# Hybrid decoder layer: projections of the third and fourth head's blocks bound to later scores, output halves interleaved

## The chip, the cores and the metric

The kernel runs on one core of a Trainium2 chip. The metric is the device time of one execution in microseconds, as the median of several executions of the same program. TensorE (PE) multiplies, VectorE (DVE), ScalarE (ACT) and GpSimd (POOL) do the element-wise work, and SyncE (SP) issues the DMA transfers.

## The reference

One layer of a decoder on a sequence of 1024 tokens of width 1024, all in float32: a joint projection, two groups of attention heads side by side, an output projection, a normalisation, and a dense SwiGLU network with its own normalisation. Cut to what matters:

```python
h = x @ w_in[l]                                    # queries, keys, values of both groups, gates
# differential attention, 4 heads: two score maps for each head
s = einsum('bqhcd,bkhcd->bhcqk', q_blk, k) * scale - slopes * dist
p = masked_softmax(s, dist >= 0)
a = p[:, :, 0] - lam * p[:, :, 1]                  # the blend of the two maps
o_diff = rms_norm(einsum('bhqk,bkhe->bqhe', a, v), subln_g) * (1 - lam_init)
o_nsa = gates[0] * o_cmp + gates[1] * o_sel + gates[2] * o_win
mix = concatenate([o_diff, o_nsa]) @ w_out[l]
x = layer_norm(DEEPNORM_ALPHA * x + mix, ln1_g[l], ln1_b[l])
ffn = (silu(x @ w_gate[l]) * (x @ w_up[l])) @ w_down[l]
x = layer_norm(DEEPNORM_ALPHA * x + ffn, ln2_g[l], ln2_b[l])
```

## The kernel before

Projections and the feed-forward products are computed in three passes: every operand is split into a high and a low part (ScalarE casts the high part on line L81, VectorE or GpSimd subtracts it on L83), and `mm3` multiplies high by high, high by low and low by high (L116 to L118). Weights that are to be split land in `big` or `w` tiles; GpSimd splits most of them.

The attention part takes about the first 600 us, and the feed-forward part the rest. In the attention part the sequence is cut into 8 blocks of 128 query rows. A unit is one block i of one head. Its **front** computes the scores of both maps against the (i + 1) * 128 keys it can see (L331 and L334, two passes into a `psS` buffer, of which there are two, up to 512 columns each), lets VectorE add the position slope, find the row's extreme value and store the result as `t` (L340), takes the exponential on ScalarE (L354, which also sums the row), and blends the two maps: VectorE inverts the row sum (L475), forms the factor (L476) and blends the first 5/8 of the columns (L478); GpSimd blends the other 3/8 (L480, L481). Its **back** transposes the blended rows in groups of four tiles (L363 into `psT`, three buffers), copies them out on ScalarE (L366, `pt`), multiplies them with the values (L493, called PV, into `psO`, one buffer) and empties `psO` twice: VectorE copies it to `od` (L497), ScalarE takes the sum of squares (L498, `ms`). After every fourth block of a head `finish` normalises the four rows (L506 to L510, with one POOL step on L509), transposes them (L513), scales them on ScalarE (L516) and sends them to DRAM (L518).

What runs beside the units is a list of **fillers**: generators that issue the projections of later heads (`qdf` for queries, `kdf` for keys, `dvf` for values), the load of the output weights (`wo_fill`) and the output projection of a block of rows (`out_fill`, two halves of 512 columns, `psM`, two buffers). They are issued at a lower priority, and a scheduler arranges each engine's instructions by priority and readiness; each engine then works through its own list in that order. The tuple of a phase in the list `phases` gives its units, its fillers, how many units' fronts go ahead of the backs (`look`), how fast fillers are spent, a priority step, and the number that becomes `passed[0]`. If that number n is set, a projection's matmul may be placed only behind the mark n + 1 from the last (`marks` collects the first score matmul of every call of `scores`); if it is None, the scheduler is free:

```python
            n = passed[0]
            if n is None or len(marks) <= n:
...
                with tc.issue_after(marks[-1 - n]):
                    mm3(*args)
```

The late phases, which the change touches, are: head 2 blocks 0 to 3, head 3 blocks 0 to 3, head 2 blocks 4 to 7 (in the order 4, 7, 6, 5), and head 3 blocks 4 to 7.

## Time and profile before

| | us |
|---|---|
| median of 3 executions | 1299.23 (1299.04 to 1299.36) |
| the profiled execution | 1298.14 |
| its span, first to last instruction | 1296.4 |
| TensorE busy | 1279.8 (99%) |
| VectorE busy | 915.7 (71%) |
| ScalarE busy | 651.2 (50%) |
| GpSimd busy | 464.5 (36%) |

A row of the timeline gives the start, the duration, engine, line, operation, output and inputs by their names in the program, the shape, and how many like instructions it holds; in brackets stands the idle time of the engine ahead of it and the instruction that ended the idle time. A row of waits gives who waited for whom, the total, the count and the longest. A row of a table by windows gives the stretch, its length, and the busy time of PE, weight loads, DVE, ACT and POOL, each with its number of instructions, then the granted clock, the share of DMA and GB/s. Matmuls are pipelined: the next one starts before the one ahead ends, so time lost is seen best from start to start.

### The profile page before, as it was taken

The page shows a single profiled execution, that of the slowest core. Times are in us where ns is not written, and L with a number is a line of the kernel's source. Part 1 is how long each engine was busy: PE and PEld are TensorE (multiplying, and loading weights), DVE is VectorE, ACT ScalarE, POOL GpSimd, SP SyncE. Part 2 cuts the span into 40 slices and gives each one's busy share as a digit, 9 for nine tenths or more (in the row PEclk, how much of TensorE's full clock was granted, in tenths as well). Part 3 has the DMA queues.
Part 4 walks back from the last instruction along what each step waited for, and adds up shares of the span by engine and source line. Part 5 has one row for each costly group of instructions (what it writes and reads, how often), then busy time and mean ns, then how long its engine had stood idle before and what let it go on. Part 6 is the DMA issues. An engine that isn't in the chain of part 4 may idle for free.

```text
span 1296.4 us, 20500 instructions
## 1 busy us (share of the span) xinstructions
PE 1279.8 (99%) x6955; PEld 1108.3 (85%) x6955; DVE 915.7 (71%) x1963; ACT 651.2 (50%) x1398; POOL 464.5 (36%) x499
## 2 busy tenths in 40 slices
PE   9999999999999999999999999999999999999997
PEld 7998999998899889788878888888888888888886
DVE  5577886677867556674797777776776768555588
ACT  5377886778766565743344233333333335433330
POOL 4434544454345355643613322322232222000071
PEclk9999999999999999999999999999999999999999
DMA  9411212021122235523224576654554559768641
GB/s 355 134 32 48 48 45 53 26 62 48 34 74 50 70 102 167 175 84 112 82 90 162 178 246 201 202 181 169 167 188 165 195 187 340 265 193 296 193 166 65
DMA packets 86841, 183.13 MB, mean 141 GB/s; under 512 B 10576, under 2 KB 19152, under 8 KB 86608
## 3 DMA queue, kind: packets, MB, share of 16 engines
q1 hardware_dynamic: 86736, 181.82, 43.4%
q8 instruction: 55, 0.90, 0.3%
q14 instruction: 50, 0.41, 0.1%
HBM read 116.18 MB, written 57.15 MB: 134 GB/s over the span
## 4 chain that ended last, share of the span: by engine, by line
PE 94%; DVE 3%; issue 1%; ACT 1%; DMA 0%; POOL 0%; DVEq 0%; ACTq 0%; POOLq 0%
PE psM L116 11%; PE psM L118 11%; PE psM L117 11%; PE psS L118 6%; PE psS L117 6%; PE psS L116 6%; PE psT L116 5%; PE psT L118 5%; PE psT L117 5%; PE psT L373 5%; PE psS L331 4%; PE psS L334 3%; PE psO L436 2%; PE psO L434 2%; PE psO L493 2%; PE psO L118 2%
## 5 line engine op out<-in xcount | busy, mean ns | idle before, releaser
L354 ACT ACTIVATE t<-t,m 128x384 f32<-128x384 f32 (+7 forms) x192 | 144.1, 752 | 59.4 <-DVE m L340 54.7
L419 POOL TENSOR_SCALAR t<-t,r,gates 128x640 f32<-128x640 f32 (+7 forms) x128 | 99.6, 783 | 166.7 <-DVE r L413 116.9
L116 PE MATMUL psM<-big,w 128*128 128x512 f32 x304 | 120.3, 396 | 0.4 <-DVE slot L171 0.3
L118 PE MATMUL psM<-big,w 128*128 128x512 f32 x304 | 119.9, 395 | 0.0
L117 PE MATMUL psM<-big,w 128*128 128x512 f32 x304 | 119.6, 394 | 0.0
L331 PE MATMUL psS<-slot,q 128*128 128x320 f32 (+10 forms) x304 | 110.7, 367 | 3.3 <-DVE m L340 2.5
L1042 POOL TENSOR_TENSOR half<-half,half 128x512 f32<-128x512 f32 x22 | 33.1, 1503 | 203.9 <-ACT half L1041 203.9
L83 DVE TENSOR_TENSOR pt<-psT,pt 128x512 fp32r<-128x512 f32 (+1 forms) x152 | 91.9, 614 | 15.4 <-ACT pt L81 14.7
L334 PE MATMUL psS<-slot,q 128*128 128x320 f32 (+10 forms) x304 | 99.3, 329 | 0.0
L81 ACT CAST pt<-psT 128x512 fp32r<-128x512 f32 (+1 forms) x152 | 77.4, 526 | 24.5 <-PE psT L373 16.5
L81 ACT CAST big<-slot 128x1024 fp32r<-128x1024 f32 (+1 forms) x54 | 54.2, 1018 | 67.5 <-DVE slot L1034 53.6
L83 DVE TENSOR_TENSOR op<-op 128x1024 fp32r<-128x1024 f32 x44 | 61.1, 1395 | 36.5 <-ACT op L81 36.1
L83 DVE TENSOR_TENSOR big<-slot,big 128x1024 fp32r<-128x1024 f32 (+1 forms) x54 | 63.8, 1187 | 29.8 <-ACT big L81 29.6
L373 PE MATMUL psT<-ident,t 128*128 128x128 f32 x528 | 83.7, 273 | 0.1
L81 ACT CAST op<-op 128x1024 fp32r<-128x1024 f32 x44 | 45.9, 1052 | 62.1 <-DMA op<-t_d 59.3
L340 DVE CUSTOM_DVE_ANT_0 t<-psS,dsel 128x384 f32<-128x384 f32 (+9 forms) x128 | 62.5, 493 | 17.3 <-PE psS L334 15.3
L1046 POOL TENSOR_TENSOR half<-half,half 128x512 f32<-128x512 f32 x22 | 36.5, 1658 | 101.5 <-DVE half L1045 101.4
L434 PE MATMUL psO<-pt,slot 128*128 128x256 f32 x264 | 72.2, 288 | 0.0
L436 PE MATMUL psO<-pt,slot 128*128 128x256 f32 x264 | 71.7, 292 | 0.0
L118 PEld LDWEIGHTS psM<-big,w 128*128 128x128 f32 x304 | 57.1, 188 | 11.5
L116 PEld LDWEIGHTS psM<-big,w 128*128 128x128 f32 x304 | 57.3, 188 | 10.7 <-DVE slot L171 0.4
L81 ACT CAST big<-big 128x1024 fp32r<-128x1024 f32 (+1 forms) x49 | 44.2, 912 | 43.4 <-DMA big<-t_d 36.9
(371 smaller groups left out, 3968.9 us busy)
## 6 DMA issues: line engine op xcount, KB each, us to landing
a_d<-slot SPq DMA_DIRECT2D x77, 256.0 KB, 3.0
t_d<-slot SPq DMA_DIRECT2D x77, 256.0 KB, 2.2
q<-q SPq DMA_DIRECT2D x48, 256.0 KB, 2.9
slot<-in_w_up_dram SPq DMA_DIRECT2D x22, 512.0 KB, 3.9
slot<-in_w_down_dram SPq DMA_DIRECT2D x22, 512.0 KB, 3.9
op<-a_d SPq DMA_DIRECT2D x44, 256.0 KB, 3.4
op<-t_d SPq DMA_DIRECT2D x44, 256.0 KB, 4.4
big<-a_d SPq DMA_DIRECT2D x33, 256.0 KB, 3.1
```

The costliest lines, as they stand in the source:

```text
L81: nc.scalar.copy(hi, src)
L83: eng.tensor_sub(lo, src, hi.bitcast(F32))
L116: nc.tensor.matmul(acc, lhsT=ah, rhs=bh, start=first, stop=False, skip_group_check=more)
L117: nc.tensor.matmul(acc, lhsT=ah, rhs=bl, start=False, stop=False, skip_group_check=more)
L118: nc.tensor.matmul(acc, lhsT=al, rhs=bh, start=False, stop=last, skip_group_check=more)
L331: mm = nc.tensor.matmul(ps[:, :c + part], lhsT=q[0], rhs=k[:, ks], start=True, stop=False)
L334: nc.tensor.matmul(ps[:, :c + part], lhsT=q[1], rhs=k[:, ks], start=False, stop=True)
L354: nc.scalar.activation(t[:, :width], t[:, :width], AF.Exp, bias=m, scale=-1.0, accum_out=r)
L373: nc.tensor.transpose(tp[:rows, n * P:(n + 1) * P], s, ident)
L419: nc.gpsimd.tensor_scalar(t, t, r[:, c:c + 1], gates[:, i, gc:gc + 1], op0=ALU.mult, op1=ALU.mult)
L434: nc.tensor.matmul(po[:, :256], lhsT=v, rhs=pt[:, 0, n * 256:(n + 1) * 256], start=False, stop=False)
L436: nc.tensor.matmul(po[:, :256], lhsT=v, rhs=pt[:, 1, n * 256:(n + 1) * 256], start=False, stop=last)
```

## The change

It has five parts. The phase of head 3, blocks 0 to 3, and the phase of head 2, blocks 4 to 7, get the number 3 for `passed[0]` in place of None, and two of the four value projections move from the first of them to the second. The blocks of head 2 run in the order 4 to 7, and `look` becomes 1 for the first of them (it was 2 and stays 2 for the rest). The output projection of rows 0 and 1 is issued as half 0 of both, then half 1 of both. The scores of block 5 of head 2 are placed behind the last PV matmul of block 3 of head 3 (`BEHIND`, `turned`). In five blocks (`WHOLE`) VectorE blends all columns and GpSimd none. Lines in the changed program stand further down: L363 stays, L475, L476 and L478 become L481, L482 and L484, L493 becomes L500, L497 and L498 become L505 and L506, L513 becomes L521.

```diff
--- before.py
+++ after.py
@@ -451,6 +451,9 @@
 
             return [make(i, kind) for i in range(NB) for kind in range(2)]
 
+        BEHIND = {(2, 5): (3, 3)}
+        WHOLE = {(3, 1), (3, 2), (3, 3), (2, 4), (2, 5)}
+        turned = {}
         late = []
 
         def diff_units(h, qt, kd, V):
@@ -469,16 +472,20 @@
                     r0, r1 = state["r0", hf][:, i4:i4 + 1], small([P, 1], "r1", 4)
                     ts.extend(t_tiles(width))
                     for c in range(2):
-                        scores(q_of(qt, i, c), kd[c], 0, width, dsel[:, 1024 - width:], slope, m[:, c:c + 1], ts[c])
+                        with ExitStack() as queued:
+                            if (h, i) in BEHIND:
+                                queued.enter_context(tc.issue_after(turned[BEHIND[h, i]]))
+                            scores(q_of(qt, i, c), kd[c], 0, width, dsel[:, 1024 - width:], slope, m[:, c:c + 1], ts[c])
                         exps(ts[c], width, m[:, c:c + 1], r1 if c else r0)
 
                     nc.vector.reciprocal(r1, r1)
                     nc.vector.scalar_tensor_tensor(r1, r0, lam[:, 0:1], r1, op0=ALU.mult, op1=ALU.mult)
-                    cut = width * 5 // 8
+                    cut = width if (h, i) in WHOLE else width * 5 // 8
                     nc.vector.scalar_tensor_tensor(ts[0][:, :cut], ts[1][:, :cut], r1, ts[0][:, :cut],
                                                    op0=ALU.mult, op1=ALU.add)
-                    nc.gpsimd.tensor_scalar(ts[1][:, cut:width], ts[1][:, cut:width], r1, None, op0=ALU.mult)
-                    nc.gpsimd.tensor_add(ts[0][:, cut:width], ts[0][:, cut:width], ts[1][:, cut:width])
+                    if cut < width:
+                        nc.gpsimd.tensor_scalar(ts[1][:, cut:width], ts[1][:, cut:width], r1, None, op0=ALU.mult)
+                        nc.gpsimd.tensor_add(ts[0][:, cut:width], ts[0][:, cut:width], ts[1][:, cut:width])
 
                 def back(fill):
                     if ("od", hf) not in state:
@@ -490,9 +497,10 @@
                         pt = transposed_whole([ts[0][:, j * P:(j + 1) * P] for j in js])
                         for n, j in enumerate(js):
                             c = (j % 4) * 256 + (h % 2) * P
-                            nc.tensor.matmul(po[:, :P], lhsT=pt[:, n * P:(n + 1) * P], rhs=V[j // 4][:, c:c + P],
-                                             start=(j == 0), stop=(j == i))
+                            av = nc.tensor.matmul(po[:, :P], lhsT=pt[:, n * P:(n + 1) * P], rhs=V[j // 4][:, c:c + P],
+                                                  start=(j == 0), stop=(j == i))
                         fill((j4 + len(js)) / (i + 1))
+                    turned[h, i] = av.ins
                     tmp = small([P, P], "ms", 2)
                     nc.vector.tensor_copy(orow[:, i4, :], po[:, :P])
                     nc.scalar.activation(tmp, po[:, :P], AF.Square, accum_out=ss[:, i4:i4 + 1])
@@ -624,14 +632,15 @@
             layer_norm(acc[i], **kw)
             nc.sync.dma_start(x1_d[i], acc[i])
 
-        def out_fill(i, normed):
+        def out_fill(i, normed, halves=(0, 1)):
             def steps():
-                out_start(i)
-                for nh in range(2):
+                if 0 in halves:
+                    out_start(i)
+                for nh in halves:
                     yield from out_half(i, nh, ps_m())
                 if normed:
                     norm1(i)
-            return steps, 10.4
+            return steps, 5.2 * len(halves)
 
         def norm_params(src, after=None):
             lnp[:] = [slot(0, F32), slot(1, F32)]
@@ -837,10 +846,11 @@
             ([(diff, 2, range(4))],
              [kdf(3, 0), kdf(3, 1), qdf(3, 0)], 2, 1.25, 130, None, False),
             ([(diff, 3, range(4))],
-             [qdf(2, 1), dvf(1, range(4, 8))], 2, 1.25, 60, None, False),
-            ([(diff, 2, (4, 7, 6, 5))],
-             [wo_fill(0), qdf(3, 1), wo_fill(1), held_fill(), out_fill(0, False), out_fill(1, False)],
-             2, 1.25, 40, None, False),
+             [qdf(2, 1), dvf(1, (4, 5))], 2, 1.25, 60, 3, False),
+            ([(diff, 2, range(4, 8))],
+             [wo_fill(0), dvf(1, (6, 7)), qdf(3, 1), wo_fill(1), held_fill(),
+              *(out_fill(i, False, (nh,)) for nh in range(2) for i in range(2))],
+             (1, 2, 2, 2), 1.25, 40, 3, False),
             ([(diff, 3, range(4, 8))],
              [ln_fill((0, 1)), out_fill(2, True), out_fill(3, True)], 2, 0.9, 60, None, False),
         ]
@@ -891,14 +901,16 @@
                 if part > 0.999:
                     run["due"] += share(work) * rate
 
-            for front, back, work, needs in units:
+            looks = look if isinstance(look, tuple) else (look,) * len(units)
+            look = looks[-1]
+            for (front, back, work, needs), ahead_of in zip(units, looks):
                 while not needs <= there:
                     assert step()
                     while run["gen"]:
                         step()
                 front()
                 pending.append((back, work))
-                while len(pending) > look:
+                while len(pending) > ahead_of:
                     finish_unit(pump, later)
             while step():
                 pass
```

How this moves instructions is shown at three places. The numbers behind the names tell buffers and tiles apart. The first place is TensorE from about 484 us on, where the backs of head 1's blocks 6 and 7 (PV into `psO_6338` and `psO_6415`) meet the scores of head 2's blocks 2 and 3 (`psS_6444`, `psS_6449`; `psS_6522`, `psS_6527`, two maps each) and of head 3's blocks 0 and 1 (`psS_6629`, `psS_6634`; `psS_6660`). Before, a query projection (`psM_6716`) and a value projection (`psM_6794`) stand among them; this is the piece around block 3's scores:

```order
L331 MATMUL psS_6522<-slot0_6018,q_6279 128x512
L334 MATMUL psS_6522<-slot0_6018,q_6279 128x512
L116 MATMUL psM_6716<-big_173,w_6135 128x512
L117 MATMUL psM_6716<-big_173,w_6135 128x512
L118 MATMUL psM_6716<-big_173,w_6134 128x512
L116 MATMUL psM_6794<-slot10_5573,big_158 128x256
L117 MATMUL psM_6794<-slot11_5574,big_158 128x256
L331 MATMUL psS_6527<-slot1_6019,q_6280 128x512
L334 MATMUL psS_6527<-slot1_6019,q_6280 128x512
L493 MATMUL psO_6415<-slot8_3030,pt_6421 128x128 x4
L493 MATMUL psO_6415<-slot9_3389,pt_6432 128x128 x4
L118 MATMUL psM_6794<-slot10_5573,big_158 128x256
```

After, from the same scores on:

```order
L331 MATMUL psS_6522<-slot0_6018,q_6279 128x512
L334 MATMUL psS_6522<-slot0_6018,q_6279 128x512
L331 MATMUL psS_6527<-slot1_6019,q_6280 128x512
L334 MATMUL psS_6527<-slot1_6019,q_6280 128x512
L500 MATMUL psO_6415<-slot8_3030,pt_6421 128x128 x4
L500 MATMUL psO_6415<-slot9_3389,pt_6432 128x128 x4
L331 MATMUL psS_6629<-slot2_6467,q_6618 128x128
L334 MATMUL psS_6629<-slot2_6467,q_6618 128x128
L331 MATMUL psS_6634<-slot4_6468,q_6619 128x128
L334 MATMUL psS_6634<-slot4_6468,q_6619 128x128
L331 MATMUL psS_6660<-slot2_6467,q_6618 128x256
L334 MATMUL psS_6660<-slot2_6467,q_6618 128x256
```

No projection stands among these scores and PV matmuls any more; the next one follows the last row shown. In the same way the eight projection matmuls ahead of the PV of `psO_6338` have moved behind it.

The second place is ScalarE at the same time. `ms_6375` is the sum of squares of `psO_6338`, which has to be read before `psO_6415` can take its place; `t_6443` is block 2 of head 2. Before:

```order
L81 CAST big_7052<-big_7052 128x512 x2
L354 ACTIVATE t_6443,r0_6379<-t_6443,m_6441 128x384
L498 ACTIVATE ms_6375,ss_6186<-psO_6338 128x128
L366 COPY pt_6432<-psT_6427 128x512
L366 COPY pt_6464<-psT_6462 128x128
L354 ACTIVATE t_6443,r1_6442<-t_6443,m_6441 128x384
```

After:

```order
L354 ACTIVATE t_6443,r0_6379<-t_6443,m_6441 128x384
L366 COPY pt_6432<-psT_6427 128x512
L81 CAST big_6947<-big_6947 128x512 x2
L366 COPY pt_6464<-psT_6462 128x128
L354 ACTIVATE t_6443,r1_6442<-t_6443,m_6441 128x384
L506 ACTIVATE ms_6375,ss_6186<-psO_6338 128x128
```

The sum of squares that empties `psO_6338` now stands behind two weight casts, two copies and two exponentials; it stood behind the casts and one exponential.

The third place is TensorE at about 520 us, where head 3's short blocks end. Before, projections (`psM_7059`) and the first map's scores of block 7 of head 2 (`psS_6948`, `psS_6953`) stand among the transposes:

```order
L493 MATMUL psO_6710<-slot6_5591,pt_6713 128x128
L331 MATMUL psS_6948<-slot0_6018,q_6786 128x512
L334 MATMUL psS_6948<-slot0_6018,q_6786 128x512
L331 MATMUL psS_6953<-slot0_6018,q_6786 128x512
L334 MATMUL psS_6953<-slot0_6018,q_6786 128x512
L117 MATMUL psM_7059<-big_173,w_6585 128x512
L118 MATMUL psM_7059<-big_173,w_6584 128x512
L116 MATMUL psM_7059<-big_173,w_6585 128x512
L513 MATMUL psT_6746<-ident_74,od_6459 128x128 x4
L363 MATMUL psT_6776<-ident_74,t_6659 128x128 x2
L363 MATMUL psT_6932<-ident_74,t_6692 128x128 x3
L117 MATMUL psM_7059<-big_173,w_6585 128x512
```

After:

```order
L521 MATMUL psT_6736<-ident_74,od_6459 128x128 x4
L363 MATMUL psT_6764<-ident_74,t_6659 128x128 x2
L363 MATMUL psT_6872<-ident_74,t_6690 128x128 x3
L363 MATMUL psT_6885<-ident_74,t_6749 128x128 x4
L500 MATMUL psO_6763<-slot6_5591,pt_6767 128x128 x2
L363 MATMUL psT_7038<-ident_74,t_6846 128x128 x4
L363 MATMUL psT_7068<-ident_74,t_6846 128x128
L500 MATMUL psO_6871<-slot6_5591,pt_6876 128x128 x3
L500 MATMUL psO_6884<-slot6_5591,pt_6890 128x128 x4
L331 MATMUL psS_6903<-slot0_6018,q_6780 128x384
L334 MATMUL psS_6903<-slot0_6018,q_6780 128x384
L331 MATMUL psS_6908<-slot0_6018,q_6780 128x384
```

Here the transposes, the PV of head 3's blocks 1, 2 and 3 (`psO_6763`, `psO_6871`, `psO_6884`) and the first map's scores of block 5 of head 2 (`psS_6903`, `psS_6908`) follow each other without a projection; a run of 19 projection matmuls (`psM_7049`) follows them.

## The prediction

> **What bounds the kernel now.** I read the page first: the shares, the slices and the chain of work that ended last.
>
> ```profile
> span 1296.4 us, 20500 instructions
> ...
> PE 1279.8 (99%) x6955; PEld 1108.3 (85%) x6955; DVE 915.7 (71%) x1963; ACT 651.2 (50%) x1398; POOL 464.5 (36%) x499
> ...
> PEclk9999999999999999999999999999999999999999
> ...
> PE 94%; DVE 3%; issue 1%; ACT 1%; DMA 0%; POOL 0%; DVEq 0%; ACTq 0%; POOLq 0%
> ```
>
> TensorE is busy for 99% of the span, at the full clock in every slice, and holds 94% of the chain. The change neither adds nor removes a matmul, so all it can move is the 16.6 us in which TensorE stands idle. Next I asked which waits of TensorE are longest, and in which stretches of 10 us around the change they lie.
>
> ```profile
> PE psS L331 <- DVE m L340: 2.5, 5, 1.1
> ...
> PE psT L513 <- DVE r L475: 1.1, 1, 1.1
> ...
> PE psO L493 <- ACT ms L498: 0.5, 1, 0.5
> ...
> PE psM L116 <- ACT slot L81: 0.3, 1, 0.3
> ```
>
> ```profile
> 480.00:490.00 10.00, 10.00 (x67) 9.05 (x66) 5.38 (x14) 8.48 (x23) 10.00 (x11) 1.00 0.45 150
> 490.00:500.00 10.00, 9.50 (x68) 8.73 (x67) 7.22 (x22) 5.69 (x17) 6.25 (x8) 1.00 0.81 213
> ...
> 520.00:530.00 10.00, 8.82 (x49) 7.03 (x48) 5.48 (x12) 8.95 (x19) 7.52 (x6) 1.00 0.66 230
> 530.00:540.00 10.00, 8.42 (x51) 6.94 (x50) 8.91 (x28) 6.34 (x17) 8.80 (x8) 1.00 0.66 182
> ...
> 640.00:700.00 60.00, 58.77 (x291) 48.28 (x291) 51.19 (x78) 30.38 (x51) 16.62 (x12) 1.00 0.27 91
> ```
>
> The first number behind the comma is TensorE's. From 480 to 500 it misses 0.50 us, from 520 to 540 it misses 1.18 + 1.58 = 2.76 us, and in the 60 us at the start of the feed-forward part 1.23 us. The order of TensorE is the same before and after up to 483.85, so the account begins there. TensorE's timeline shows where the 2.76 us lie, in the long blocks of heads 2 and 3:
>
> ```profile
> 527.37 0.37 PE L334 MATMUL psS<-slot,q 128*128 128x448 f32 x1
> 528.84 0.47 PE L331 MATMUL psS<-slot,q 128*128 128x448 f32 x1 [1.10 <-DVE m L340]
> ...
> 536.29 0.34 PE L334 MATMUL psS<-slot,q 128*128 128x384 f32 x1
> 537.11 1.16 PE L493 MATMUL psO<-slot,pt 128*128 128x128 f32 x8 [0.49 <-ACT ms L498]
> ...
> 538.55 0.31 PE L334 MATMUL psS<-slot,q 128*128 128x320 f32 x1
> 539.96 0.63 PE L513 MATMUL psT<-ident,od 128*128 128x128 f32 x4 [1.09 <-DVE r L475]
> ```
>
> Matmuls overlap, so I count lost time from start to start. From 527.37 to 528.84 are 1.47 us for a matmul whose turn takes about 0.20, so 1.27 are lost, 0.17 more than the idle time shown (the refill behind a wait). The other two lose 0.65 and 1.26 in the same way. Together 3.2 us.
>
> **What the change removes.** All three waits stand where the order of before has few projections left. In the new order 18 projection matmuls come between the two maps of block 5's scores, 11 before block 6's, and 2 to 12 stand between one pair of scores and the next, 0.23 us each: mostly 1.4 to 2.8 us of cover, against 1.3 for the longest wait. So I take the 3.2 us away, and with them 1.0 of the small restarts that the same stretch pays behind switches between scores and transposes (an estimate: some ten restarts of 0.1). **Minus 4.2.** The cover is gone if ScalarE or VectorE is late by more than about 1.5 us; the first rival is that.
>
> **What it adds, place A (484 to 496).** The projections that stood among the scores of head 2's blocks 2 and 3 are now held back behind the first scores of block 1 of head 3. What is left for TensorE is attention work whose steps wait for one another. These are the rows that set its pace:
>
> ```profile
> 483.62 0.39 PE L118 MATMUL psM<-big,w 128*128 128x512 f32 x1
> 483.85 0.40 PE L116 MATMUL psM<-big,w 128*128 128x512 f32 x1
> ...
> 485.69 1.06 PE L493 MATMUL psO<-slot,pt 128*128 128x128 f32 x8
> 486.51 0.42 PE L331 MATMUL psS<-slot,q 128*128 128x384 f32 x1
> ```
>
> ```profile
> 485.24 0.16 DVE L475 RECIPROCAL r<-r 128x1 f32<-128x1 f32 x1 [2.91 <-ACT t L354]
> 485.44 1.01 DVE L476 SCALAR_TENSOR_TENSOR r<-r,lam,r 128x1 f32<-128x1 f32 x1
> 486.49 1.38 DVE L478 SCALAR_TENSOR_TENSOR t<-t,r 128x160 f32<-128x160 f32 x1
> 487.79 0.74 DVE L177 SCALAR_TENSOR_TENSOR q<-psM,qscale,q 128x512 fp32r<-128x512 f32 x1
> 488.45 0.55 DVE L340 CUSTOM_DVE_ANT_0 t<-psS,dsel 128x384 f32<-128x384 f32 x1
> ...
> 496.61 0.22 DVE L476 SCALAR_TENSOR_TENSOR r<-r,lam,r 128x1 f32<-128x1 f32 x1
> ...
> 496.86 0.55 DVE L478 SCALAR_TENSOR_TENSOR t<-t,r 128x320 f32<-128x320 f32 x1
> ```
>
> ```profile
> 486.82 1.29 ACT L81 CAST big<-big 128x512 fp32r<-128x512 f32 x2
> 489.04 0.62 ACT L354 ACTIVATE t<-t,m 128x384 f32<-128x384 f32 x1 [0.92 <-DVE m L340]
> ...
> 489.65 0.26 ACT L498 ACTIVATE ms<-psO 128x128 f32<-128x128 f32 x1
> 489.81 0.19 ACT L498 ACTIVATION_READ_ACCUMULATOR ms<-psO 128x1 f32 x1
> 489.90 0.74 ACT L366 COPY pt<-psT 128x512 f32<-128x512 f32 x2
> ...
> 493.64 0.71 ACT L354 ACTIVATE t<-t,m 128x512 f32<-128x512 f32 x1
> ```
>
> TensorE's work from 483.85 to the first held projection: 30 PV passes of 0.11, two for each matmul (8 took 0.82 in the row at 485.69), 4 scores of 384 columns at 0.17, 4 of 512 at 0.23, 4 of 128 and 4 transposes at 0.11, 2 of 256 at 0.12: 6.0 us. The waits, by the durations of before, with what each engine now has in front:
> 1. TensorE is free at 486.55. The first scores of 512 columns need a score buffer, which L340 of 384 columns frees. VectorE is in L476 and L478 until 487.79, then 0.55: 488.35. Wait 1.8.
> 2. The second scores of 512 need the other buffer: L177 (0.66 to the next start), then L340 again, 489.6. TensorE is there at 488.9. Wait 0.7.
> 3. The PV of head 1's block 7 needs psO, which L498 on ScalarE frees. In front of L498 now stand, from 488.4 on: exp of 384 (0.61 to the next start), copy, two casts L81 (1.29), copy (0.62 for both copies), exp of 384 (0.61), then L498 itself: 491.8 to 492.1. TensorE is there at 490.15. Wait 1.7 to 1.9.
> 4. After 16 PV passes and four scores of 128, at 494.2, the scores of 256 wait for L340 of 128 columns, which VectorE reaches only behind reciprocal, L476, L478 of 320 columns and L497, all of them behind two exps of 512 (0.71 each): 494.8 to 495.2. Wait 0.6 to 0.9.
> With four refills of 0.1 that is 5.2 to 5.7 lost, 5.4 taken. Before, the same stretch lost 1.1: the 0.50 idle of the row 490 to 500, its refill, and some restarts. **Plus 4.3.** Lower bound: L476 and L478 run as at 496.61 and 496.86 (0.22 and under 0.5) and the first three waits begin 1.8 earlier, so plus 2.5. Upper bound: one more hold of VectorE of 1.0 ahead of wait 4, plus 5.3.
>
> The row at 485.44 is an operation on one column that takes 1.01 us, against 0.22 later. While it runs, POOL is in the split of weights:
>
> ```profile
> 482.64 5.04 POOL L83 TENSOR_TENSOR big<-big 128x512 fp32r<-128x512 f32 x4
> ```
>
> The Trainium skill (SBUF — State Buffer, section "SBUF: two separate sides") says that VectorE with two inputs in SBUF and GpSimd exclude each other for a whole instruction. By that rule the 1.01 and 1.38 are waits for one split of 1.26 each, and as POOL's order is unchanged here, they come again and the sum stays; without it they would be 0.22 and 0.4, and the sum 1.8 lower. The trace agrees with the rule.
>
> **Place B (about 520).** Head 3's short blocks end with 12 entries without a projection between them: transposes, PV of three blocks through the single psO, and a transposed output row. Their work is about 4 us; psO must be emptied twice by L498 (a PV there cost 0.49 idle in the row at 537.11, 0.65 lost), and a transpose buffer once by a copy or by L516. Two waits of 0.3 to 0.6 and one of 0.5: **plus 1.4**, between 0.5 and 2.2.
>
> **Place C (about 525 to 535).** The output rows' casts and splits now stand with weight casts on ScalarE, but beside 12 or more projections: **plus 0.3**, from 0 to 2 (first rival).
>
> **What costs nothing.** Blends of five blocks go to VectorE alone: 3/8 more columns, at most 0.3 us on an engine that is 71% busy; ten POOL instructions go. BEHIND puts the scores of head 2's block 5 right behind the last PV of place B, where TensorE is late anyway. Output halves in turn need the same loads and matmuls; SP's queue has the same DMAs in another order, its bound is in place C. The waits of 0.3 in the row 640 to 700 stay, plus or minus 1.
>
> **Sum.** -4.2 + 4.3 + 1.4 + 0.3 = +1.8 us. The profiled execution's own time is 1298.14 us, span 1296.4 and 1.74 around it, 1.09 under the median of three runs, 1299.23; the sum gives 1299.9 for such an execution and **1301.0** for the median. 0.2% (2.6 us) is about what a measurement of this kernel can tell from no change: faster is under 1296.6, slower over 1301.8.
>
> **Rivals.**
> - *Slower: a stall of ScalarE or VectorE returns in the long blocks.* The 1.10 us wait came of one row:
>
> ```profile
> 526.40 1.71 DVE L83 TENSOR_TENSOR w<-w 128x512 fp32r<-128x512 f32 x1 [1.17 <-ACT w L81]
> ```
>
>  VectorE waits 1.17 for the cast, then is held 1.71. The cast can stand behind weight casts that wait for a DMA. If this costs once more what it cost before (1.27) or up to 2, the net is +3.1 to +3.8, 1302.3 to 1303.0, and with place A at its upper bound 1304. It decides from 0.8 us of such a wait. For: four weight casts stand in a row on ScalarE in the new order, too. Against: projections beside it. Chance 0.30.
> - *Faster: the held projections cost nothing, as the short blocks flow better alone.* Then waits 1 and 2 fall (POOL's splits end before VectorE's blend), the rest begins 1.8 earlier, and the casts in wait 3 find their place behind L498 (1.29 less): place A adds 1.2, B 0.5, and the net is -2.5; with the idle of 1.23 at 640 to 700 partly gone, -3, 1296.2. Against it stand the rows at 482.64 and 486.82, which nothing here moves. It decides if A loses under 2 us in all. Chance 0.15.
> - *The clock falls in place A.* TensorE would idle 5 of 11.4 us there, in pieces of at most 1.9. At the very start the first matmuls run slow:
>
> ```profile
> 2.36 3.78 PE L690 MATMUL psO<-ident 128*128 128x128 f32 x16 [2.36 <-POOL ident masks.py:199]
> 5.80 0.77 PE L116 MATMUL psS<-big,w 128*128 128x512 f32 x1
> ```
>
>  16 passes there take 3.44 to the next start, 0.21 each, where 0.11 is usual: 1.7 us lost. As much again would give 1302.7. Waits of 1.1 with 1.00 granted (row 520 to 530) speak against it. Chance 0.05. The Trainium skill (TensorE: Matmul & The Clock Gate, section "HAM oscillation — how this bites in real kernels") puts the limit at an idle gap of about 3.4 us; by that rule place A stays at full speed, and no run here shows such a gap.
> - *Nothing moves*: the bound holds back what would have waited anyway. The order speaks against it, since 8 projections stood at 484 to 486; it would give 1299.2 and lies inside "same".
>
> **Chances.** The forecast with its bounds, and the last rival: 0.50, "same". Slower: 0.30 + 0.05 = 0.35. Faster: 0.15. The range reaches from 1296.9 (most of "faster" left out, 0.12) to 1304.2 (A and C both at the upper end beyond it, 0.06).
>
> **What would show it.** In the changed profile: waits of psS on L340, psO on L498 and psS on L340 between 486 and 496, 5 us in all, none over 2; about 1.4 us near 520; TensorE over 9.8 of 10 us in each stretch from 524 to 545. If the stretch 484 to 496 idles under 2 us, the faster rival holds; if waits over 0.8 us stand between 524 and 545, the slower one.

## The result, and the profile after

The changed kernel takes 1311.2 us, the median of four executions (1309.62 to 1312.81), against 1299.13 (1298.69 to 1299.36) for the kernel before on the same chip: a ratio of 1.0093 [1.0076, 1.0111], slower by 12 us. The profiled execution took 1309.62 us, 11.5 more than the one of before. Its page, in the lines that answer to those of before:

```profile
span 1307.9 us, 20485 instructions
...
PE 1284.2 (98%) x6955; PEld 1109.8 (85%) x6955; DVE 914.5 (70%) x1963; ACT 653.4 (50%) x1398; POOL 459.3 (35%) x489
...
PEclk9999999999999999999999999999999999999999
...
PE 88%; DVE 4%; issue 3%; DMA 2%; POOL 2%; ACT 1%; SPq 0%; DVEq 0%; ACTq 0%; POOLq 0%
```

TensorE works through the same 6955 matmuls, but its share of the chain fell from 94% to 88%, and a DMA now has 2% of it. By the page the clock is at full speed in each of the 40 slices; a slice is 33 us, and shorter falls do not show in its digits. Among the longest waits of TensorE:

```profile
PE psS L331 <- DVE m L340: 3.8, 7, 1.7
PE psO L500 <- ACT ms L506: 2.5, 3, 1.4
...
PE psT L948 <- DVE half L967: 1.4, 1, 1.4
```

The waits that were to go (psS on L340 at 528.84, psO on the sum of squares, psT on the reciprocal) have others in their place. The table by windows, with the first number behind the comma for TensorE and the granted clock third from the right:

```profile
480.00:490.00 10.00, 8.31 (x61) 7.39 (x59) 4.90 (x15) 7.25 (x17) 9.99 (x11) 1.00 0.53 178
490.00:500.00 10.00, 6.84 (x33) 5.65 (x32) 6.64 (x27) 5.80 (x22) 6.52 (x8) 0.83 0.65 179
520.00:530.00 10.00, 8.54 (x68) 7.87 (x67) 3.36 (x11) 6.04 (x21) 0.50 (x1) 1.00 0.67 234
530.00:540.00 10.00, 10.00 (x53) 8.62 (x53) 4.53 (x14) 6.09 (x15) 6.23 (x6) 1.00 0.56 186
540.00:550.00 10.00, 8.29 (x46) 6.70 (x45) 8.22 (x16) 6.84 (x13) 5.97 (x4) 1.00 0.72 211
...
640.00:700.00 60.00, 56.98 (x286) 46.31 (x285) 52.48 (x79) 28.15 (x47) 20.45 (x15) 1.00 0.23 84
```

Between 480 and 500 TensorE idles 4.85 us, against 0.50 before, and 490 to 500 has a granted clock of 0.83. From 530 to 540 it is busy throughout, as was meant; the idle time has moved to 520 and to 540. TensorE's timeline shows place A, place B, place C and the start of the feed-forward part:

```profile
489.55 0.50 PE L331 MATMUL psS<-slot,q 128*128 128x512 f32 x1 [1.69 <-DVE m L340]
...
490.68 0.50 PE L331 MATMUL psS<-slot,q 128*128 128x512 f32 x1 [0.41 <-DVE m L340]
...
492.83 3.63 PE L500 MATMUL psO<-slot,pt 128*128 128x128 f32 x16 [1.41 <-ACT ms L506]
497.51 0.30 PE L331 MATMUL psS<-slot,q 128*128 128x128 f32 x1 [1.06 <-DMA q<-q]
...
524.47 0.66 PE L363 MATMUL psT<-ident,t 128*128 128x128 f32 x4 [0.39 <-ACT tmp L524]
...
526.42 0.94 PE L500 MATMUL psO<-slot,pt 128*128 128x128 f32 x6 [0.29 <-ACT ms L506]
528.14 1.05 PE L500 MATMUL psO<-slot,pt 128*128 128x128 f32 x7 [0.79 <-ACT ms L506]
...
542.04 0.85 PE L363 MATMUL psT<-ident,t 128*128 128x128 f32 x6 [0.70 <-DVE t L484]
...
544.30 0.50 PE L116 MATMUL psM<-big,w 128*128 128x512 f32 x1 [1.01 <-DVE q L177]
...
667.71 0.63 PE L948 MATMUL psT<-ident,half 128*128 128x128 f32 x4 [1.36 <-DVE half L967]
```

The first three waits of place A are the forecast ones in place, and a little shorter: 3.51 us together, where 4.2 to 4.4 were forecast. The fourth is not: it ends with a DMA. And the 16 PV passes ahead of it take 0.23 us each, twice the 0.11 of elsewhere. Counted from start to start against the usual turn of each matmul, TensorE loses in the two profiled executions:

| stretch, us | before | after | forecast difference | difference |
|---|---|---|---|---|
| 0 to 20 | 2.4 | 3.4 | 0 | +1.0 |
| 480 to 500 (place A) | 1.0 | 7.8 | +4.3 | +6.8 |
| 520 to 560 (B, C, the removed waits) | 4.8 | 4.8 | -2.5 | 0 |
| 660 to 700 | 2.7 | 5.0 | 0 | +2.3 |
| 500 to 520 and 600 to 620 | 0.4 | 1.2 | 0 | +0.8 |

The differences add up to 10.9 of the 11.5 us. The first 20 us are the same code and lose 2.6 to 3.5 us in the other kernels' profiles, so that line is not the change's.

**The DMA.** A query projection writes the rows of both maps into one tile, and `evac_q` rearranges them with three copies between partitions (L161). The third writes rows that the other two read first. The tile's view for q, 480 to 500 us, with the first and last issue and the times to landing:

```profile
L161 SPq DMA_DIRECT2D q<-q x3: 462/467/605, 490.2 to 494.4; - x3
...
DMA to landing us min/median/max: 2.9/3.0/3.7
```

From VectorE's scaled row (L177, done about 490.2) to the first scores of head 3 there are thus two landings in a row, 3.7 us for the second copy and 3.0 for the third, to about 497.4: some 7 us. TensorE's wait for them ends at 497.51.

**The clock.** The granted clock changes only at steps of 3.41 us. Place A in windows set on these steps:

```profile
485.92:489.34 3.42, 1.94 (x16) 1.63 (x14) 2.48 (x4) 2.42 (x6) 3.42 (x4) 1.00 0.45 156
489.34:492.75 3.41, 1.46 (x4) 0.59 (x4) 2.96 (x12) 3.22 (x11) 2.77 (x4) 1.00 0.44 94
492.75:496.16 3.41, 3.33 (x15) 3.33 (x16) 2.48 (x5) 1.43 (x5) 3.22 (x4) 0.50 0.48 101
496.16:499.57 3.41, 2.07 (x13) 1.64 (x12) 1.52 (x11) 1.19 (x7) 0.76 (x1) 1.00 0.94 310
```

TensorE is idle for 1.95 of the 3.41 us from 489.34, and the next step is granted at 0.50. Here the loss costs little, since the slow PV ends in the wait for the DMA anyway. VectorE's timeline, for what holds place A, place C and the feed-forward part:

```profile
487.67 1.35 DVE L484 SCALAR_TENSOR_TENSOR t<-t,r 128x160 f32<-128x160 f32 x1
488.94 0.54 DVE L340 CUSTOM_DVE_ANT_0 t<-psS,dsel 128x384 f32<-128x384 f32 x1
...
539.88 2.02 DVE L484 SCALAR_TENSOR_TENSOR t<-t,r 128x768 f32<-128x768 f32 x1
...
542.36 1.23 DVE L83 TENSOR_TENSOR w<-w 128x512 fp32r<-128x512 f32 x1
543.51 0.74 DVE L177 SCALAR_TENSOR_TENSOR q<-psM,qscale,q 128x512 fp32r<-128x512 f32 x1
...
665.55 1.41 DVE L663 SCALAR_TENSOR_TENSOR slot<-slot,mv,slot 128x512 f32<-128x512 f32 x2
666.88 0.68 DVE L967 TENSOR_TENSOR half<-slot,slot 128x512 f32<-128x512 f32 x1
```

The blend at 539.88 is late because of ScalarE too: the exponential that the reciprocal ahead of it waits for starts at 537.38, behind casts that wait for the DMA of the output weights:

```profile
536.27 1.21 ACT L81 CAST big<-big 128x512 fp32r<-128x512 f32 x2 [0.89 <-DMA big<-wo_d]
```

### The profile page after: what moved, and what is told of

It is laid out like the page before. It is cut to its first block, busy times and chain, and to the rows that moved or that the text cites. A ratio compares the mean times of both kernels' runs of the same rounds, so it can differ in the third digit from the quotient of the medians.

```text
span 1307.9 us, 20485 instructions
## 1 busy us (share of the span) xinstructions
PE 1284.2 (98%) x6955; PEld 1109.8 (85%) x6955; DVE 914.5 (70%) x1963; ACT 653.4 (50%) x1398; POOL 459.3 (35%) x489
## 4 chain that ended last, share of the span: by engine, by line
PE 88%; DVE 4%; issue 3%; DMA 2%; POOL 2%; ACT 1%; SPq 0%; DVEq 0%; ACTq 0%; POOLq 0%
PE psM L116 10%; PE psM L117 10%; PE psM L118 10%; PE psT L116 5%; PE psT L118 5%; PE psT L117 5%; PE psS L118 5%; PE psS L116 5%; PE psS L117 5%; PE psT L373 5%; PE psS L331 4%; PE psS L334 3%; PE psO L436 2%; PE psO L434 2%; PE psO L116 2%
## 5 line engine op out<-in xcount | busy, mean ns | idle before, releaser
L340 DVE CUSTOM_DVE_ANT_0 t<-psS,dsel 128x384 f32<-128x384 f32 (+9 forms) x128 | 62.5, 493 | 21.4 <-PE psS L334 19.2
L116 PEld LDWEIGHTS psM<-big,w 128*128 128x128 f32 x304 | 57.2, 188 | 12.3 <-DVE q L177 1.4
L331 PEld LDWEIGHTS psS<-slot,q 128*128 128x128 f32 x304 | 57.4, 189 | 11.5 <-DVE m L340 6.2
```

The costliest lines, as they stand in the source:

```text
L116: nc.tensor.matmul(acc, lhsT=ah, rhs=bh, start=first, stop=False, skip_group_check=more)
L331: mm = nc.tensor.matmul(ps[:, :c + part], lhsT=q[0], rhs=k[:, ks], start=True, stop=False)
```

## The experiments

The theory after the result: the first bound (`passed[0]` = 3 in head 3's short blocks) empties place A of projections and costs most of the 12 us, partly through the query copies and the clock. The rivals: BEHIND, the moved value projections, the whole blends or the output halves cost it; or place A's price is one single wait. All times are set against the kernel before on the same chip; it took 1299.01 to 1299.13 us on the chips used, so experiments can be compared with each other too; a reader can follow the sums in the table behind the last experiment.

**1. The first bound alone undone.**

```diff
-             [qdf(2, 1), dvf(1, (4, 5))], 2, 1.25, 60, 3, False),
+             [qdf(2, 1), dvf(1, (4, 5))], 2, 1.25, 60, None, False),
```

> The changed kernel with the first of the two bounds undone: the phase of head 3, blocks 0 to 3, gets None again for passed[0]; all else as changed. The projections stand among the scores and PV of 484 to 496 again. If place A is the main loss (its profile lost 7.8 us from 480 to 500 against 1.0 before), this takes 6.5 to 7 us off a profiled run, and if the halved clock seen there (0.83 granted from 490 to 500) is what spreads the changed kernel's runs from 1309.6 to 1312.8, the runs of this one lie within 1 us of each other, at 1302 to 1304, with a granted clock of 0.999 in each. If the clock has another cause, the spread of 3 us stays. If the loss lies mainly in the tail and at 520 to 545, the time stays over 1306.

Measured: 1303.17 us (1301.65 to 1304.48), ratio 1.0031 [1.0020, 1.0043]. The time is as expected, the spread of 2.8 us is not (1 was). Place A is back to 1.0 us lost. The bound costs 8.0 us in this setting, and 4 us are left to something else. The largest wait left is in place C, and it is the first rival of the prediction as it was written: ScalarE's casts wait for the DMA of the output weights, VectorE's split waits for a cast, and TensorE for a result behind it. ScalarE, VectorE and TensorE in turn:

```profile
533.00 0.63 ACT L81 CAST big<-big 128x512 fp32r<-128x512 f32 x1 [1.39 <-DMA big<-wo_d]
```

```profile
535.68 1.34 DVE L83 TENSOR_TENSOR w<-w 128x512 fp32r<-128x512 f32 x1 [1.16 <-ACT w L81]
536.95 0.74 DVE L177 SCALAR_TENSOR_TENSOR q<-psM,qscale,q 128x512 fp32r<-128x512 f32 x1
```

```profile
537.74 0.50 PE L116 MATMUL psM<-big,w 128*128 128x512 f32 x1 [2.21 <-DVE q L177]
```

Behind it the clock falls for one step, which here lies on projections. They start every 0.43 us in it, where 0.23 is usual, so about half of the step, 1.7 us, is lost (an estimate):

```profile
535.61:539.02 3.41, 1.28 (x6) 1.07 (x7) 3.15 (x6) 3.12 (x7) 3.06 (x3) 1.00 0.80 229
539.02:542.43 3.41, 3.41 (x10) 2.69 (x9) 0.69 (x1) 1.33 (x4) 0.39 (x1) 0.50 0.95 244
```

```profile
539.39 0.63 PE L116 MATMUL psM<-big,w 128*128 128x512 f32 x1
539.82 0.63 PE L117 MATMUL psM<-big,w 128*128 128x512 f32 x1
```

**2. The first wait filled.** Nine unused matmuls of 384 columns run in the first wait of place A; they add work and change no result.

```diff
+            for _ in range(idle):
+                nc.tensor.matmul(tp[:, P:512], lhsT=k[:, 0:P], rhs=k[:, 0:384], start=True, stop=True)
...
-                        pt = transposed_whole([ts[0][:, j * P:(j + 1) * P] for j in js])
+                        pt = transposed_whole([ts[0][:, j * P:(j + 1) * P] for j in js], 9 if (h, i) == (2, 0) else 0, kd[0])
```

> The changed kernel with nine matmuls of 384 columns more, behind the transpose of head 2's block 0, into columns of its psT buffer that nothing reads: about 1.6 us of TensorE work in the place where it waited 1.69 us for the first scores of 512 columns. They add work and remove no wait. Theory clock (the idle stretches of place A halve TensorE's clock, in some executions for longer): the clock stays at 1.00 in the profile from 484 to 500, the mean granted clock is 0.998 to 0.999 in all runs, the spread shrinks to 1 us, and the median falls by 1 to 2.5 us, to 1309 to 1310. Theory waits (only what TensorE waits for counts, the clock is an effect without a price): the median stays at 1311, or rises by up to 0.3, and the spread stays.

Measured: 1309.55 (1308.22 to 1310.61), 1.0080 [1.0066, 1.0094]; the interval overlaps that of the change. In the profile the first wait fell to 0.38, but the waits of 0.40 and 1.24 behind it and what was left of the first put 1.94 us of idle time into one step, and the clock fell from 492.61 to 496.03 all the same. The experiment did not take the fall away, so it does not price it; that its median lies in the range of the clock theory supports nothing.

**3. The third query copy left out** for the tile that head 3's first scores read. The scores then read rows that were not moved.

```diff
-            move(q[0][64:128, :], q[0][0:64, :])
+            if third:
+                move(q[0][64:128, :], q[0][0:64, :])
...
-                    evac_q(q, qscale[:, n - 4:n - 3], ps)
+                    evac_q(q, qscale[:, n - 4:n - 3], ps, (n, hf) != (14, 0))
```

> The changed kernel without the third of the three DMAs that spread the first half of head 3's queries over partitions (the copy of rows 0 to 63 of q to rows 64 to 127); the scores of head 3's blocks 0 to 3 are then computed with other numbers. The third DMA waits until the first two have read its target. Theory DMA chain (in the changed kernel the scores of head 3's block 0 waited to 497.51 for that copy, and PV at half speed ended inside that wait): the scores start up to 2.8 us earlier, and a run with full clock gains 2 to 2.8 us, one with half clock 1.0. Median 1308.5 to 1310. Theory engines (the wait is VectorE's and ScalarE's, as in the prediction's schedule): no change, under 0.5 us.

Measured: 1308.55 (1307.59 to 1310.41), 1.0070 [1.0056, 1.0084]; 2.65 us under the change, whose interval it just touches. TensorE's timeline has no wait for a DMA any more:

```profile
492.35 3.78 PE L501 MATMUL psO<-slot,pt 128*128 128x128 f32 x16 [0.58 <-ACT ms L507]
495.79 0.45 PE L332 MATMUL psS<-slot,q 128*128 128x128 f32 x1
```

The chain of copies is a real wait: the scores of 128 columns start at 495.79, 1.7 us earlier than in the change. Its whole price does not come back, since the PV ahead of the scores still runs at the half clock, and the clock is low for two steps (489.99 to 496.82).

**4. Output halves in pairs again.**

```diff
-              *(out_fill(i, False, (nh,)) for nh in range(2) for i in range(2))],
+              out_fill(0, False), out_fill(1, False)],
```

> The changed kernel with the output projection of rows 0 and 1 as before: both halves of row 0, then both of row 1. If the interleaving is what delays the rows' normalisation and so the start of the feed-forward part (TensorE lost 5.0 us from 660 to 700, 2.7 before, 1.36 of it in one wait for the differences of rows), this takes 1.5 to 2.5 us off. If the delay is that all of the output projections end later, it takes under 0.5 off, or costs up to 1 where the halves had covered a wait at 530 to 545.

Measured: 1312.48 (1310.59 to 1314.07), 1.0103 [1.0089, 1.0116]. The stretch 660 to 700 still loses 4.9 us. The interleaved halves are not the cause.

**5. The third copy left out, and idle time filled** with unused matmuls: the edits of 2 and 3 together.

```diff
-            move(q[0][64:128, :], q[0][0:64, :])
+            if third:
+                move(q[0][64:128, :], q[0][0:64, :])
...
+            for _ in range(idle):
+                nc.tensor.matmul(tp[:, P:512], lhsT=k[:, 0:P], rhs=k[:, 0:384], start=True, stop=True)
```

> The kernel without the third query move (e3) plus the nine matmuls without use of e2. In e3's profile TensorE's clock stood at half for two periods of 3.41 us from 489.99 on and for one from 544.61. Theory clock by share of idle (a period of 3.41 us that idles over about 1.6 us is followed by one at half clock; the four profiles so far fell at 1.65, 1.88, 1.90, 1.94, 1.96, 2.13 and 2.38 us idle and did not at 1.54, 1.48 and below): with the first wait filled the period that ended at 489.99 idles under 0.9 us, so at most one period at half clock follows in place A; the median is 1 to 2.5 us under e3's 1308.55, at 1306 to 1307.6. Theory waits alone: same as e3, within 0.5, or up to 0.3 over it.

Measured: 1308.12 (1306.26 to 1312.2), 1.0073 [1.0059, 1.0087], not to be told from 3, and over the 1306 to 1307.6 expected. In its profile place A has one slow step in place of two, as expected, but waits of 1.87 and 1.0 in place C bring two slow steps there. Inconclusive.

**6. All four value projections back in the first phase, which is then without its bound.**

```diff
-             [qdf(2, 1), dvf(1, (4, 5))], 2, 1.25, 60, 3, False),
+             [qdf(2, 1), dvf(1, range(4, 8))], 2, 1.25, 60, None, False),
...
-             [wo_fill(0), dvf(1, (6, 7)), qdf(3, 1), wo_fill(1), held_fill(),
+             [wo_fill(0), qdf(3, 1), wo_fill(1), held_fill(),
```

> The changed kernel with the first bound undone and all four value projections back in the phase of head 3's short blocks; what stays of the change is the second bound, the order 4 to 7, look, BEHIND, WHOLE and the halves in turn. If the 4 us that e1 still loses against before come from the two value projections that stand later (the work that covered the last output rows then stands in the middle), the loss at 660 to 700 falls from 4.9 to under 3.5 us and the time to 1299 to 1301. If they come from the second bound and the whole blends, it stays at 1302 to 1304, with the wait on L177 behind 530 and the loss from 660 to 700 as in e1.

Measured: 1305.87 (1304.8 to 1306.42), 1.0049 [1.0035, 1.0063]: over both expectations and worse than 1 by 2.7, with a wait of 1.67 on L518 and a slow step at place B, and 5.0 us lost from 660 to 700. The moved values do not cost the 4 us that 1 left over. Taking them back costs 2.7 here, while moving them costs 2.7 in 15, so their price hangs on the rest of the kernel.

**7. The second bound alone**, in the kernel before: the 3 that was to remove the three waits.

```diff
-             2, 1.25, 40, None, False),
+             2, 1.25, 40, 3, False),
```

> The kernel before with one number changed: 3 in place of None for the phase of head 2's long blocks, so that its projections are bound to scores; no value projection moved, order 4, 7, 6, 5, blends and halves as before. The prediction's minus 4.2 us is the price of the waits this is meant to cover. If the bound alone covers them, the stretch 520 to 545 loses under 1.5 us (4.8 before) and the time is 1295 to 1297. If projections only change places with waits, it stays within 1 us of 1299.0.

Measured over 11 executions: 1298.94 (1298.3 to 1300.33), 1.0001 [0.9993, 1.0010]. The stretch 520 to 560 loses 4.9 us, against 4.8 before. In place of the three waits, six of 0.23 to 0.46 stand between 534 and 543:

```profile
530.00:540.00 10.00, 8.85 (x48) 6.40 (x46) 8.37 (x25) 6.76 (x18) 8.69 (x8) 1.00 0.68 178
540.00:550.00 10.00, 9.14 (x63) 7.94 (x64) 7.42 (x25) 7.67 (x18) 4.25 (x4) 1.00 0.34 113
```

**8. Blends shared with GpSimd again.**

```diff
-        WHOLE = {(3, 1), (3, 2), (3, 3), (2, 4), (2, 5)}
+        WHOLE = set()
```

> The changed kernel with WHOLE empty: GpSimd blends 3/8 of the five blocks again. Theory: the whole blends keep VectorE (2.02 us for 768 columns beside a split of weights on GpSimd) from emptying psM at 544, so without them the wait on L177 falls by 0.6 to 1 us and the median by 0.5 to 1.5. Rival: the wait is ScalarE's, whose casts wait for a DMA of the output weights and stand ahead of the cast that VectorE's split needs; then the median stays within 0.7 of 1311.2, or rises by 1 to 2, as GpSimd's share of a blend stands behind splits of 1.26 us.

Measured: 1317.7 (1317.09 to 1319.77), 1.0146 [1.0133, 1.0160]. Without whole blends the changed kernel takes 6.5 us more, and neither theory forecast that. The wait on L177 did fall, from 1.01 to 0.32. But the profile has slow steps from 492.95 to 503.19 and a new wait in the feed-forward part, on a cast that itself waits for a DMA of attention output, with slow steps around it (TensorE, then ScalarE):

```profile
631.02 0.80 PE L116 MATMUL psS<-big,w 128*128 128x512 f32 x1 [3.59 <-ACT w L81]
```

```profile
630.35 0.62 ACT L81 CAST w<-w 128x512 fp32r<-128x512 f32 x1 [3.98 <-DMA w<-mix_d]
```

From 620 to 640 TensorE loses 7.8 us, against 0.2 in the change, which is more than the whole difference. How the shared blends of five earlier blocks make that DMA late is not shown.

**9. The first half of the output weights loaded behind place A**, so that neither its casts nor its splits stand in front of place A's steps. Small copies on VectorE make the load wait.

```diff
+                    if (h, i) == (3, 0):
+                        turned["od"] = orow
...
-                    wo[nh, kp] = load_split_here(wo_d[nh, kp], *big_tiles(), l_eng="pool", order=(0, 1))
+                    hi, lo = big_tiles()
+                    if nh == 0:
+                        for part in (0, 512):
+                            nc.vector.tensor_copy(lo[:, part:part + 1], turned["od"][:, 0, 0:1])
+                    wo[nh, kp] = load_split_here(wo_d[nh, kp], hi, lo, l_eng="pool", order=(0, 1))
```

> The changed kernel with the first half of the output weights loaded later: each of its eight pieces waits (through a column that VectorE writes into its target) for the first output row of head 3, so that ScalarE's casts and GpSimd's splits of these weights fall behind place A. Theory (the prediction's first and third wait: VectorE's blends held by GpSimd's splits, ScalarE's sum of squares behind two casts): the first wait falls from 1.7 us to under 0.3, the query DMAs start 1.5 to 1.9 us earlier, and place A loses 3.5 to 4.5 us in place of 7.8; with fewer periods at half clock the median falls by 3 to 5 us, to 1306 to 1308. If the splits come too late for the output projection, 1 to 2 us of that are given back between 525 and 560. Rival (the chain of scores, exponentials and PV is the limit by itself): place A still loses over 6 us.

Measured: 1306.1 (1305.24 to 1308.25), 1.0055 [1.0041, 1.0068]; 5.1 us under the change, as expected. TensorE's waits in place A:

```profile
489.04 2.05 PE L502 MATMUL psO<-slot,pt 128*128 128x128 f32 x16 [0.36 <-ACT ms L508]
...
493.95 0.30 PE L331 MATMUL psS<-slot,q 128*128 128x128 f32 x1 [2.85 <-DMA q<-q]
```

The waits for VectorE are gone and that for ScalarE is 0.36, so casts and splits of the weights together were their cause. What is left is the wait for the query copies, now 2.85 in plain sight; 480 to 500 still loses 4.1. Waits of 1.15 and 0.21 for splits at 536 and 539 give some of it back.

**10. The last row's normalisation behind the last differences** of the feed-forward part, so that L663 no longer stands ahead of L967 on VectorE.

```diff
-        nc.vector.tensor_sub(t2, b22, b11)
+        last = nc.vector.tensor_sub(t2, b22, b11)
...
+        sums.append(last.ins)
...
-    norm1(7, vector_only=True)
+    with tc.issue_after(sums[-1]):
+        norm1(7, vector_only=True)
```

> The changed kernel with one order fixed at the start of the feed-forward part: the last row's normalisation is placed behind the differences of the row ahead (the second of them, L967, stood behind the normalisation's first steps in the changed order of VectorE, and ahead of them in the order of before). Theory: the wait of 1.36 us on L967 goes, or falls under 0.3, the loss from 660 to 700 falls from 5.0 to 3.5 us, and the median by 1 to 1.5, to 1309.8 to 1310.2. Rival (the last rows are late as a whole): the wait moves to the next transposes and the median stays within 0.5.

Measured: 1309.92 (1308.66 to 1311.11), 1.0081 [1.0067, 1.0095]. The wait of 1.36 on L967 became one of 0.20, and others took its place: 660 to 700 loses 5.2. The median lies where it was expected, but the interval overlaps that of the change and the stretch lost no less, so this is luck. What makes that stretch slow is not settled by it.

**11. The kernel before with the order 4 to 7 and the second bound.**

```diff
-            ([(diff, 2, (4, 7, 6, 5))],
+            ([(diff, 2, range(4, 8))],
...
-             2, 1.25, 40, None, False),
+             2, 1.25, 40, 3, False),
```

> The kernel before with two parts of the change: head 2's long blocks in the order 4 to 7, and the bound 3 for their phase. If the order of the blocks takes away the waits at 528 to 542 (the longest block came second before), this is the version that beats both: 1296 to 1298. If the waits move with the blocks, it is 1298 to 1300; if it brings the clusters of place B with it, 1300 to 1303.

Measured over 11 executions: 1298.19 (1297.43 to 1299.37), 0.9992 [0.9983, 1.0000]. The stretch 520 to 560 loses 3.3 us. The best version of all, by less than can be told from no change with certainty.

**12. The change without the first bound and without BEHIND.**

```diff
-        BEHIND = {(2, 5): (3, 3)}
+        BEHIND = {}
...
-             [qdf(2, 1), dvf(1, (4, 5))], 2, 1.25, 60, 3, False),
+             [qdf(2, 1), dvf(1, (4, 5))], 2, 1.25, 60, None, False),
```

> The changed kernel without the first bound and with BEHIND empty: the scores of head 2's block 5 may stand ahead of the last PV of head 3's block 3 again. Theory: the cluster of place B (about 2.2 us lost in e1) comes of the scores held back, so it falls under 1 us and the median to 1301 to 1302.2, against 1303.2 for e1. Rival: the cluster comes of the second bound and the order of blocks, and the median stays at 1302.7 to 1303.7.

Measured over 11 executions: 1299.19 (1298.14 to 1300.45), 1.0000 [0.9991, 1.0009]: the time of before, 2 us under what was expected. Place B has no wait, and 640 to 700 idles as before:

```profile
520.00:530.00 10.00, 10.00 (x53) 8.44 (x53) 6.39 (x14) 8.41 (x20) 6.50 (x5) 1.00 0.91 311
...
640.00:700.00 60.00, 58.75 (x291) 48.19 (x290) 52.25 (x80) 30.39 (x51) 16.79 (x12) 1.00 0.27 93
```

Against 1, which differs in BEHIND alone, this is 4.0 us less.

**13. BEHIND alone undone**, the first bound kept.

```diff
-        BEHIND = {(2, 5): (3, 3)}
+        BEHIND = {}
```

> The changed kernel with BEHIND empty, the first bound kept. If the two costs add up, this takes 4 us off, to 1306.7 to 1307.7, with place A as in the changed kernel (7 to 8 us lost from 480 to 500), and no cluster near 520. If place A's delay by itself makes the later waits, it stays over 1309.

Measured: 1310.33 (1307.34 to 1312.96), 1.0077 [1.0064, 1.0091], only 0.9 less than the change. The two parts do not add. The profiled execution is the slowest of the five; the fastest, 1307.34, had a mean clock of 0.997 against its 0.992. It has four slow steps in a row at place A: TensorE is idle 0.94 and 0.89 us in the first two of them, and 0.09 in the third, behind which one more follows all the same. The step ahead of them and the first of them:

```profile
487.98:491.39 3.41, 1.41 (x8) 0.72 (x7) 3.38 (x8) 2.20 (x6) 3.39 (x4) 1.00 0.19 71
491.39:494.81 3.42, 2.48 (x8) 1.76 (x9) 2.84 (x8) 3.42 (x12) 2.79 (x3) 0.50 0.73 153
```

The last slow step ends at 505.05, among projections, where a slow step costs 1.7 us.

**14. BEHIND in the kernel of 11**, with `look` as in the change.

```diff
+        BEHIND = {(2, 5): (3, 3)}
...
-             2, 1.25, 40, 3, False),
+             (1, 2, 2, 2), 1.25, 40, 3, False),
```

> The kernel before with the order 4 to 7, the second bound, look (1, 2, 2, 2) and BEHIND, and nothing else of the change (all values early, blends shared, halves of a row together). e11 is the same without look and BEHIND, at 1298.2. Theory: BEHIND costs 4 us by itself, 1301.5 to 1303.5, with a cluster of waits near 515 to 525 and 4 to 5 us lost from 660 to 700. Rival: it costs only where values are moved too, then 1298 to 1299.5.

Measured: 1304.71 (1304.2 to 1306.09), 1.0044 [1.0032, 1.0057]: 6.5 us over 11, more than the 4 expected. Place B by TensorE's timeline:

```profile
517.25 0.63 PE L521 MATMUL psT<-ident,od 128*128 128x128 f32 x4 [1.67 <-DVE od L518]
518.81 1.12 PE L363 MATMUL psT<-ident,t 128*128 128x128 f32 x4 [0.39 <-ACT tmp L524]
...
523.42 1.16 PE L500 MATMUL psO<-slot,pt 128*128 128x128 f32 x8 [0.78 <-ACT ms L506]
```

There is also a slow step from 518.40 and a wait of 1.90 at 543, and 660 to 700 loses 4.9 us, as in the change. BEHIND (with `look`) brings place B and the loss at 660 to 700 without the rest of the change; in 12, `look` without BEHIND does not.

**15. Two value projections moved, in the kernel of 11.**

```diff
-             [qdf(2, 1), dvf(1, range(4, 8))], 2, 1.25, 60, None, False),
+             [qdf(2, 1), dvf(1, (4, 5))], 2, 1.25, 60, None, False),
...
-             [wo_fill(0), qdf(3, 1), wo_fill(1), held_fill(), out_fill(0, False), out_fill(1, False)],
+             [wo_fill(0), dvf(1, (6, 7)), qdf(3, 1), wo_fill(1), held_fill(), out_fill(0, False), out_fill(1, False)],
```

> e11 (order 4 to 7 and the second bound) with two of the four value projections moved behind the load of the output weights, as in the change. Theory: 5.2 us of projections more to put among the long blocks; the stretch 520 to 545 loses under 1.5 us (e11 3.0) and the time falls to 1296.5 to 1297.7. Rival: what is covered there is missing elsewhere, 1298 to 1299.5.

Measured: 1300.86 (1300.28 to 1302.79), 1.0016 [1.0007, 1.0025]: 2.7 us over 11 and over both expectations, with waits of 1.21 and 1.20 near 541 and one slow step.

One way through the runs that accounts for the 12 us:

| step | from, to | us |
|---|---|---|
| order 4 to 7 and second bound | before, 11 | -0.9 |
| values moved, look, halves, whole blends | 11, 12 | +1.0 |
| BEHIND | 12, 1 | +4.0 |
| first bound | 1, after | +8.0 |

By the other way, the first bound costs 11.1 (12 to 13) and BEHIND 0.9 on top of it (13 to after).

## Why the prediction was wrong

The time lies above the range, 10 us over the forecast of 1301.0. The profiled execution took 9.7 us more than the 1299.9 of the sum; by the table of stretches 2.5 of that lie in place A, 2.5 from 520 to 560, 2.3 from 660 on, 0.8 at 500 to 520 and 600 to 620, and 1.0 in the first 20 us, which the change does not touch. By the steps of the sum:

- **Place A, +4.3: the mechanism of waits 1 to 3 was right; what stands behind them was left out.** Waits 1 to 3 were forecast as 1.8, 0.7 and 1.7 to 1.9, and measured 1.69, 0.41 and 1.41. Experiment 9 shows their cause to be the forecast one, casts and splits of weights in front of the needed steps (L484 of 160 columns took 1.35 us beside a split, as the row of before had it). Wait 4, scores of 256 columns behind L340, was forecast as 0.6 to 0.9 and measured 0.28. Ahead of it stand two things that were not in the account: the wait of 1.06 for the query copies, some 7 us of DMA, and the PV at the half clock, which took 3.63 us for 16 passes where before took 1.95. In 9, at the full clock, the wait for the copies is 2.85. The copies are in the trace of before: the third, issued at 492.8, took 2.9 us, and a score of 128 columns waits 0.50 until 495.84. That profile puts the wait down to a VectorE copy of `od`, which ended at about the same time; in the kernels of 1, 7, 11, 12, 14 and 15, with TensorE's order of before there, the same wait of 0.51 to 0.73 bears the DMA's name. The bound holds the projections until just these scores have been issued, and so leaves nothing to cover the copies. The stretch lost 6.8 more in place of 4.3.
- **The clock, a rival at 0.05: it happened**, in the change and in most of its relatives. The prediction looked at each wait by itself ("in pieces of at most 1.9"). The runs show that idle time counts in sum over a step of 3.41 us, so that in the change the last 0.2 us of the first wait, 0.41 and 1.33 of the third do it together. The steps do not begin at the same place of the program in each execution, which fits the spread of 3 to 6 us within one kernel: the change's executions of 1309.62 and 1312.81 us have mean clocks of 0.998 and 0.993.
- **The removal, -4.2: not there as a gain.** The three waits did go, and 530 to 540 is busy throughout. But with the second bound alone (7) the time is that of before, and with the order (11) it is 0.9 better. From 520 to 560 TensorE loses 4.8 us before, 4.8 after and 4.9 in 7. Of the 4.8 after, places B and C hold 2.0 each, so what was to go did go, about 4.0 of the 4.8, and B and C, forecast as 1.7 together, took all of it back. Cover was counted for the three waits one by one; the waits changed places. Why they must (the late results come from ScalarE's and VectorE's lists, which the bound does not shorten) is argued, not shown.
- **Place B, +1.4, was right within its bounds**: 0.39, 0.29 and 0.79 of idle time, 2.0 lost, forecast 0.5 to 2.2. **Place C, +0.3, was too low**: 2.0, the upper end given. The first rival, casts that wait for a DMA, was seen in 1, and in the change as the cast at 536.27; behind it VectorE took 2.02 us for a blend of 768 columns, and TensorE waited 0.70 for that and 1.01 for L177. By the prediction's own sign, a wait over 0.8 between 524 and 545, this rival held, but its price of up to 2 us explains only a part.
- **BEHIND at nothing: wrong by 4.0 to 6.5 us** in settings without the first bound (12 and 1, 11 and 14), and by 0.9, which is within the noise, on top of it (13). "TensorE is late anyway" was the step that failed: scores that stand behind the last PV of place B cannot fill its waits, and by 12 and 14 place B is there when BEHIND is, and gone without it.
- **The stretch 640 to 700, plus or minus 1: +2.3.** It goes with BEHIND (2.7 lost in 12, about 4.9 in 1, 4 and 14); 13, with the first bound and without BEHIND, lies between, at about 3.7. In the change a row's normalisation (L663, 1.41) has slipped ahead of the difference that TensorE waits for (L967); 10 shows that this one row is not all of it. How BEHIND reaches so far is open; that it shifts the last rows' normalisation on VectorE is argued, not shown.
- **Whole blends at nothing: the changed kernel is 6.5 us slower without them (8).** By the loss from 620 to 640 that is the wait at 631, and its way from the blends is not shown; in place C the whole blend itself is what TensorE waited 0.70 for.

The time by which the clock rival would have gone, 1302.7, was low as well, since its price was added to a sum that already lacked the copies, BEHIND and the stretch from 640 on.

## What to carry to other kernels

Before a bound keeps filler work behind a mark, ask what the marked instruction itself waits for, its DMA chain too: until then nothing covers it. A wait for several things bears one name, so look at when each of the inputs was ready. Where an engine is 99% busy, add the idle time of neighbouring waits over a few microseconds before calling them small, and do not book a removed wait as a gain until the part has run by itself.

## What the runs showed of the hardware

The granted clock of TensorE was 1.00 or 0.50, in steps of 3.41 us whose grid lies otherwise in each execution. Over all profiles here, up to the idle end of each program, 18 steps at the full clock were followed by one at half; TensorE was idle 1.64 to 2.42 us in them, often in several waits. No step with up to 1.54 us idle was followed by a fall; two, with 1.64 and 1.84, kept the full clock all the same (in the profiles of 10 and 9). Five of the 18 had no single wait over 1.25, and the 1.64 and 1.84 were single waits, so the sum over the step tells more than the longest wait. From half, the clock came back behind steps with up to 0.38 us idle, with one exception under 0.1 (in 13), and stayed low behind eight of nine steps with 0.72 to 1.53. The Trainium skill (TensorE: Matmul & The Clock Gate, section "HAM oscillation — how this bites in real kernels") sets a gap of about 3.4 us as the limit: the length of the step agrees, but here about half a step of idle time was enough, and the measurement decides.

In the change the three copies of q between partitions ahead of head 3's first scores took 2.9 to 3.7 us from issue to landing, and about 7 us together, since the third was issued only when the first two had landed.
